# Stationary columns, transpose order and fills in a hand-ordered two-layer decoder kernel

## Chip, cores and metric

The kernel runs on one core of a Trainium2 chip. The metric is device time in microseconds (us) for one launch; lower is better. Engines are named as in the profile: PE is TensorE's matmul side and PEld its weight loads, DVE is VectorE, ACT is ScalarE, POOL is GpSimd, SP is SyncE, which issues the DMAs.

## What is computed

512 tokens and 16 learned meta tokens in front of them (528 rows of width 1024) pass a gated linear attention layer and a differential softmax attention layer. Each layer has an RMS norm, one input projection, a gate and an output projection; a last norm drops the meta rows. The change sits mostly in the first layer, whose core is this (cut from the reference):

```python
def gla_chunk(S, inp):
    q, k, v, lg = inp
    b = jnp.cumsum(lg, axis=2)
    ...
    attn = jnp.einsum('bhid,bhjd,bhijd->bhij', q, k, decay)
    o = (jnp.einsum('bhij,bhjv->bhiv', attn, v)
         + jnp.einsum('bhid,bhdv->bhiv', q * jnp.exp(b), S))
...
q, k, v, z, g_lr = jnp.split(proj, ...)
lg = jax.nn.log_sigmoid((g_lr @ w_gate_up + b_gate)) / GLA_TAU
...
o = head_rms(o) * gnorm
y = jax.nn.silu(z) * o
return y @ w_out
```

There are four heads with keys of 256 and values of 512. In the second layer eight heads of 2 x 128 take a softmax over earlier tokens with a relative bias, the difference of two softmaxes weighs the values, and the same norm, gate and output projection follow.

## The kernel before, in words

**Layout.** Activations lie transposed, features on the 128 partitions and tokens along the row. The 528 tokens are one meta block of 16 and four blocks of 128 (`BLK`). Projections are done in float32r with each operand split in a high and a low part (`split`, L237: ACT copies the high part, DVE subtracts it from the source), three products each. From the second head on, the projections use a seven-product scheme on 2 x 2 blocks (`Unit`, L362); head 0 uses `plain_unit` (L739).

**The order of the work.** PE's order is written out by hand; the other engines are ordered by a scheduler that keeps dependences and favours functions marked `urgent`. `Weaver` (L73) holds a queue of generators, the projections. Each yields the microseconds that it is taken to cost: `Unit` yields 0.33 after three products, `plain_unit` 0.66 after six, the output projection (L821) 0.68 after six. `W.fill(us)` runs yields until their sum reaches `us`; in that way projections are put between the steps of the attention, so that PE has work while DVE and ACT prepare the next step. `W.defer(us, fn)` keeps `fn` until yields of that sum have passed. `W.finish` empties the queue up to `W.stop`, `W.settle` runs what is still deferred. `Weights` (L129) loads weight pieces with SP and has ACT and DVE split them; it looks two pieces ahead.

**One head of the first layer.** `gla_scores` (L1011) scales the keys into `kd` on DVE, multiplies the meta block's keys and queries (L1023, the "meta scores"), then the four diagonal blocks (L1030). Four calls of `gla_cross` (L1038, called from `gla_ready`, L1059, with a fill of 1.5 between) multiply each block's queries by the earlier blocks' keys: at L1048, for each earlier block `j` two products, `j = 0` being the meta block. These score products are in float32; each is carried out as two matmul instructions. L1052 then scales `kd` by the block's decay on DVE. `gla_blocks` (L1066) multiplies the scores by the values (`output`), norms them, and `rows` (L1105) transposes the rows back at L1111.

**Values.** A finished projection tile of the values has features on partitions and has to be turned: `turned_back` (L758) defers a `post` that calls `to_tokens` (L730). That makes one transpose of a 32-column tile for the meta rows (L734) and four of 128 columns (L736), in two tiles of a PSUM pool of four (`ps_tile`). The copies out of them are `split` and `split3` (L328; L333, L334 on ACT, L336, L338 on DVE). `to_tokens` is used by the second layer too (`turned_back2`, L1379), and there the 32-column transposes of the probabilities (L1487) come after the 128-column ones (L1486).

**The branch.** If a decay is very steep, scores are made in another way (`steep_scores`). Whether that is so is found once: DVE reduces the decays to a flag `fl` (L908, L909), a one-column product on PE (L1130, the "steepness product") carries it to PSUM, DVE casts it to `fi` (L1131), and all engines load it and branch (L1133, L1134). The fills around it are at L1128 and L1132. With these inputs the branch is not taken. At that place the queue holds head 0's plain projections of q and k and behind them its gate projection.

Of the kernel before, what the change touches and what calls it, by code (L numbers as in the profile page):

```python
# [19 lines left out]
P = 128  # L20
D = 1024
NM = 16
# [162 lines left out]
def trunk(ctx, tc, x, meta, g_norm, gla_w_in, gla_w_gate_up, gla_b_gate, gla_gnorm, gla_w_out,  # L185
# [3 lines left out]
    act, dve, pe, pool, sp = nc.scalar, nc.vector, nc.tensor, nc.gpsimd, nc.sync  # L189
# [17 lines left out]
    def T(p, shape, dt, tag, **kw):  # L207
        uid[0] += 1
        return p.tile(shape, dt, tag=tag, name=f"{tag}_{uid[0]}", **kw)
# [10 lines left out]
    def ps_tile():  # L220
        return T(ps_pool, [P, 512], F32, "ps")
# [4 lines left out]
    def h2(t):  # L226
        return t.rearrange("p (a b) -> p a b", a=2)
# [44 lines left out]
    W = Weaver()  # L272
# [14 lines left out]
    def want_unit(w, c0):  # L287
        def single(tag, b):
            def fn(raw):
                t = [T(wp, [P, 512], F32R, tag + part, bufs=1) for part in "hl"]  # L290
                split(*t, raw[:, b, :])
                return t
            return Part(tag, fn)

        def add(o, a, b):
            dve.tensor_tensor(o, a, b, op=ALU.add)

        def sums(raw):
            t = T(wp, [P, 2, 512], F32, "sum", bufs=1)
            add(t[:, 1, :], raw[:, 2, :], raw[:, 3, :])  # L300
            add(t[:, 0, :], t[:, 1, :], raw[:, 0, :])
            add(raw[:, 2, :], raw[:, 2, :], raw[:, 0, :])
            return t

        def outer(raw):
            add(raw[:, 1, :], raw[:, 1, :], su.t[:, 0, :])
            ws.room["sum"] += 1
            return block_pair(raw[:, 1:3, :])

        a11, a12, a22 = single("a11", 0), single("a12", 1), single("a22", 3)  # L310
        su = Part("sum", sums)
        s21 = Part("pair", lambda raw: block_pair(su.t))
        s43 = Part("pair", outer)
        ws.want((w, c0), [a11, su, s21, a12, s43, a22])
        return a11, a12, a22, s21, s43
# [174 lines left out]
    def tmp():  # L490
        return T(tp, [P, L], F32, "t")
# [16 lines left out]
    ident = cp.tile([P, P], F32, name="ident")  # L508
# [90 lines left out]
    pm = pm0[:, :KT * NM].rearrange("p (k m) -> p k m", k=KT)  # L599
# [50 lines left out]
    for k0 in range(0, KT, 2):  # L650
        if k0 + 2 < KT:
            scaled_pair(k0 + 2)
        i, ks = k0 // 4, slice(k0 % 4, k0 % 4 + 2)
# [76 lines left out]
    def to_tokens(vt, blocks, short_cols):  # L730


        pt, pm = ps_tile(), ps_tile()[:32, :P]
        pe.transpose(pm, short_cols, ident)  # L734
        for b, (t0, n) in enumerate(blocks[1:]):
            pe.transpose(pt[:, b * P:(b + 1) * P], vt[:, t0:t0 + n], ident)  # L736
        return pt, pm

    def plain_unit(u, evac):  # L739
# [15 lines left out]
    def q_gla_v(hd, s):  # L755
        us = [want_unit(g_w_in, 2048 + 512 * hd + c) for c in (0, 256)] if hd else v_first

        def turned_back(m, vt):  # L758
            def post():
                pt, pm = to_tokens(vt, BLK, vt[:, :32])  # L760
                cs = slice(m * P, (m + 1) * P)
                split(s.v[0][:, :, cs], s.v[1][:, :, cs], pt.rearrange("p (b c) -> p b c", b=4))
                split3(s.vm[:, cs], pm, 32, short[:, NM:NM + 1])
            W.defer(1.4, post)

        gens = []
        for h, u in enumerate(us):
            vts = []

            def dst(h=h, vts=vts):  # L770
                if h == 0:
                    s.vm = T(gp, [M3, 512], F32R, "vm0")
                    s.v = [T(gp, [P, 4, 512], F32R, f"v{i}") for i in range(2)]
                vts.extend([tmp(), tmp()])
                return vts

            if hd:
                gens.append(W.add(Unit(u, X, 1.0, dst, lambda i, h=h, vts=vts: turned_back(2 * h + i, vts[i]))))
            else:
                def evac(i, banks, h=h, vts=vts, dst=dst):  # L780
                    if i == 0:
                        dst()
                    for n, bank in enumerate(banks):
                        act.activation(vts[i][:, n * HT:(n + 1) * HT], bank[:, :HT], AF.Copy)
                    turned_back(2 * h + i, vts[i])

                gens.append(W.add(plain_unit(u, evac)))
        return gens[0]
# [59 lines left out]
    for k in range(KT):  # L848
        for n in range(2):
            for i, x in enumerate((X["b11"], b12) if k < 4 else (X["b21"], X["b22"])):  # L850
                pe.matmul(pgs[i][:112, :HT], glr[:, k, :], x[n][:, k % 4, :],
                          start=k == 0 and n == 0, stop=k == KT - 1 and n == 1)
# [157 lines left out]
    @urgent  # L1010
    def gla_scores(hd, s):  # L1011
        s.a = [T(gp, [P, NR], F32R, f"a{i}") for i in range(2)]
        s.kd = T(gp, [P, 2, 400], F32, "kd")
        for i in range(2):
            dve.tensor_scalar(s.kd[:, i, :NM], s.ks[:, i, :NM], eL[:, 2 * hd + i, 0:1], None, op0=ALU.mult)
            dve.tensor_tensor(s.kd[:, i, NM:].rearrange("p (b c) -> p b c", b=3),
                              s.ks[:, i, NM:400].rearrange("p (b c) -> p b c", b=3),
                              eL[:, 2 * hd + i, 1:4].unsqueeze(2).to_broadcast([P, 3, P]), op=ALU.mult)
        sp.dma_start(s.kd, steep_dr[hd][1], cond=steep > 0, cond_hint=False)
        s.am = T(gp, [M3, NM], F32R, "am")  # L1020
        pm = ps_tile()[:32, :NM]
        for i in range(2):
            pe.matmul(pm, s.ks[:, i, :32], s.qs[:, i, :NM], start=i == 0, stop=i == 1)  # L1023
        r = tmp()
        dve.tensor_tensor(r[:32, :NM], pm, short[:, :NM], op=ALU.mult)
        ps = ps_tile()
        for b in range(4):
            cs = slice(NM + b * P, NM + (b + 1) * P)
            for i in range(2):
                pe.matmul(ps[:, b * P:(b + 1) * P], s.ks[:, i, cs], s.qs[:, i, cs], start=i == 0, stop=i == 1)  # L1030
        dve.tensor_tensor(r[:, NM:].rearrange("p (b c) -> p b c", b=4), ps.rearrange("p (b c) -> p b c", b=4),
                          tri.unsqueeze(1).to_broadcast([P, 4, P]), op=ALU.mult)
        sp.dma_start(r, steep_dr[hd][0], cond=steep > 0, cond_hint=False)
        split3(s.am, r[:32, :NM], 64)
        split(s.a[0], s.a[1], r[:, NM:])

    @urgent
    def gla_cross(hd, s, b):  # L1038


        t0, n = BLK[b]
        ps, w = ps_tile(), (b - 1) * P
        pm = ps[:32, 384:]
        for j in range(b):
            c0 = BLK[j][0]
            o, kc = (ps[:, (j - 1) * P:j * P], slice(c0, c0 + P)) if j else (pm, slice(0, 32))
            for i in range(2):
                pe.matmul(o, s.kd[:, i, kc], s.qs[:, i, t0:t0 + n], start=i == 0, stop=i == 1)  # L1048
        if b < 4:
            for i in range(2):  # L1050
                kd = s.kd[:, i, :t0]
                dve.tensor_scalar(kd, kd, eL[:, 2 * hd + i, b:b + 1], None, op0=ALU.mult)  # L1052
        cs = slice((b - 1) * P, b * P)
        split3(s.cm[:, cs], pm, 64)
        if b > 1:
            cs = slice(w * (b - 2) // 2, w * b // 2)
            split(s.c[0][:, cs], s.c[1][:, cs], ps[:, :w])
# [67 lines left out]
        W.fill(2.0)  # L1125
        rows(4, prev)

    W.fill(1.0)  # L1128
    pf = ps_tile()
    pe.matmul(pf[0:1, 0:1], fl[:, 1:2], one1, start=True, stop=True)  # L1130
    dve.tensor_copy(fi, pf[0:1, 0:1])  # L1131
# [11 lines left out]
    for hd in range(G_HEADS):  # L1143
        s = heads[hd]
        last = hd == G_HEADS - 1
        if hd:
            if not last:
                q_gla_out(hd - 1, heads[hd - 1])
            for half in range(2):
                q_gla_z(hd, s, half)  # L1150
            if not last:
                W.stop = q_gla_qk(hd + 1, heads[hd + 1])[0]
            if hd == 1:
                second_layer_setup()
            W.fill(4.0)
        if hd == 0:
            W.fill(2.0)
        gla_scores(hd, s)
        W.fill(5.0)
        gla_ready(hd, s)  # L1160
        if hd == 0:
            hot = T(gp, [P, TLEN], F32, "kd")
            sp.dma_start(hot[:NBUCK + 1], c_hot)
        W.finish()
        W.settle()
        if hd == 0:
            for m in range(4):
                gla_gate(0, s, m, h2(s.z[:, m, :]))
        if hd == 0:
            q_gla_qk(1, heads[1])  # L1170
        W.stop = None
        if last:
            q_gla_out(hd - 1, heads[hd - 1])
        else:
            W.stop = q_gla_v(hd + 1, heads[hd + 1])
        gla_blocks(hd, s, (1.2, 1.2) if last else (1.7, 1.5), last)
        W.finish()
        W.stop = None

# [427 lines left out]
    s = heads[0]  # L1607
# [14 lines left out]
    for hd in range(D_HEADS):  # L1622
        last = hd == D_HEADS - 1
        s = heads[hd]
# [112 lines left out]
```

## Time and profile before

| | |
|---|---|
| median of 3 timed runs | 1003.09 us (1002.08 to 1003.71) |
| the profiled execution, first to last instruction | 999.6 us |
| the profiled execution's time beyond that span | not recorded apart; the timed median is 3.5 us above the span |
| granted TensorE clock, mean | 0.997 |
| first layer in the timeline | to about 480 us; second layer from there |
| instructions | 18267 |

In a row of the timeline the columns are the start in us, the busy time, engine, line and operation, output and inputs, shape and the number of merged instructions; a bracket gives the idle time ahead of it and what ended that. For a matmul the first shape (128*32) is the stationary operand, partitions by columns, and the second the moving one. Matmuls are pipelined: a single one lasts longer than the distance to the next, so of n merged ones the last starts one duration ahead of the row's end. In a row of the waits the columns are the total in us, how often, and the longest. A row that groups the instructions of one line gives their count and the minimum, median and maximum duration in ns.

### The profile page before, as it was taken

The numbers are of one execution on the slowest core, as the hardware profiler recorded it, in microseconds if no ns is written. First come the engines' busy times: TensorE is split into PE (matmuls) and PEld (weight loads), VectorE is DVE, ScalarE is ACT, GpSimd is POOL, SyncE is SP. The second block draws the span as 40 slices with busy tenths as digits, with TensorE's granted clock in tenths as the row PEclk, the third lists the DMA queues.
The fourth block names the chain that finished last, engine by engine and source line by source line (L and its number), as shares of the span: only waits on it lengthen the run. The fifth ranks groups of instructions, "written<-read, shape, count | busy, mean of one in ns | idle before, by whom it ended". The sixth has DMA issues, their size and how long they took to land.

```text
span 999.6 us, 18267 instructions
## 1 busy us (share of the span) xinstructions
PE 981.0 (98%) x7143; PEld 920.2 (92%) x7143; DVE 784.1 (78%) x1586; ACT 597.5 (60%) x1304; POOL 46.6 (5%) x68
## 2 busy tenths in 40 slices
PE   8999999999999999999999999999999999999997
PEld 6998999999999989999899898899998999988896
DVE  7998886777777787556998886888966879777785
ACT  7775755265535656536567666466664666645583
POOL 1000000001000100000000100000010010000001
PEclk9999999999999999999999999999999999999998
DMA  7322322141233322222231322333222332323212
GB/s 194 82 69 64 86 85 86 48 113 52 85 85 85 85 54 74 86 85 79 84 104 49 94 82 95 85 96 85 85 96 72 87 91 70 109 64 92 85 65 84
DMA packets 121161, 84.24 MB, mean 84 GB/s; under 512 B 6365, under 2 KB 110077, under 8 KB 121072
## 3 DMA queue, kind: packets, MB, share of 16 engines
q1 hardware_dynamic: 121072, 83.05, 28.8%
q8 instruction: 56, 0.92, 0.4%
q14 instruction: 33, 0.27, 0.1%
HBM read 83.64 MB, written 2.12 MB: 86 GB/s over the span
## 4 chain that ended last, share of the span: by engine, by line
PE 78%; DVE 6%; ACT 3%; DMA 3%; issue 1%; POOL 1%; SPq 0%; POOLq 0%; DVEq 0%; ACTq 0%
PE bx L357 15%; PE bx L347 10%; PE bv L357 9%; PE by L357 8%; PE ps L326 7%; PE bx L830 4%; PE bx L326 3%; PE bv L830 2%; PE by L830 2%; DMA raw<-in_gla_w_in_dram 2%; PE ps L1048 2%; PE by L326 2%; PE bv L326 2%; DVE wl L241 1%; PE by L347 1%
## 5 line engine op out<-in xcount | busy, mean ns | idle before, releaser
L240 ACT ACTIVATE wh<-raw 128x1024 fp32r<-128x1024 f32 x99 | 104.4, 1055 | 61.6 <-PE by L830 26.8
L241 DVE TENSOR_TENSOR wl<-raw,wh 128x1024 fp32r<-128x1024 f32 x99 | 121.0, 1222 | 22.0 <-ACT wh L240 14.6
L357 PE MATMUL bv<-x,wh 128*128 128x264 f32 (+1 forms) x656 | 97.5, 286 | 0.0
L357 PE MATMUL bx<-x,wh 128*128 128x264 f32 (+1 forms) x640 | 95.6, 286 | 1.2 <-ACT u L378 1.2
L357 PEld LDWEIGHTS bx<-x,wh 128*128 128x128 f32 x640 | 84.8, 188 | 2.3 <-ACT u L378 1.4
L357 PEld LDWEIGHTS bv<-x,wh 128*128 128x128 f32 x656 | 86.4, 189 | 0.3
L241 DVE TENSOR_TENSOR wl<-sum,wh 128x1024 fp32r<-128x1024 f32 x41 | 50.1, 1222 | 21.0 <-ACT wh L240 17.6
L378 ACT ACTIVATE u<-bx 128x264 f32<-128x264 f32 (+1 forms) x120 | 45.5, 380 | 33.1 <-PE bx L357 29.2
L347 PE MATMUL bx<-x,wh 128*128 128x512 f32 (+1 forms) x256 | 62.4, 385 | 0.0
L1473 ACT ACTIVATE p<-p,st 128x528 f32<-128x528 f32 (+3 forms) x64 | 36.4, 569 | 40.0 <-DVE st L1471 39.9
L357 PE MATMUL bv<-x,wl 128*128 128x264 f32 (+1 forms) x328 | 56.4, 286 | 0.0
L240 ACT ACTIVATE wh<-sum 128x1024 fp32r<-128x1024 f32 x41 | 43.2, 1055 | 19.2 <-PE by L830 9.6
L357 PE MATMUL bx<-x,wl 128*128 128x264 f32 (+1 forms) x320 | 54.5, 285 | 0.0
L347 PEld LDWEIGHTS bx<-x,wh 128*128 128x128 f32 x256 | 44.5, 188 | 7.9
L1509 POOL TENSOR_TENSOR st<-st,mhalf 128x1 f32<-128x1 f32 x32 | 26.5, 828 | 474.9 <-ACT on L1507 426.9
L357 PE MATMUL by<-x,a12h 128*128 128x264 f32 (+1 forms) x320 | 46.9, 285 | 0.0
L357 PEld LDWEIGHTS bv<-x,wl 128*128 128x128 f32 x328 | 46.2, 189 | 0.0
L357 PE MATMUL bx<-x,a11h 128*128 128x264 f32 (+1 forms) x320 | 46.2, 285 | 0.0
L357 PEld LDWEIGHTS bx<-x,wl 128*128 128x128 f32 x320 | 45.3, 188 | 0.1
L240 ACT ACTIVATE a11h<-raw 128x512 fp32r<-128x512 f32 x41 | 25.7, 628 | 32.6 <-DMA raw<-in_diff_w_in_dram 18.2
L357 PEld LDWEIGHTS bx<-x,a11h 128*128 128x128 f32 x320 | 42.2, 189 | 0.8
L357 PEld LDWEIGHTS by<-x,a12h 128*128 128x128 f32 x320 | 41.9, 188 | 0.2 <-issue 0.2
(465 smaller groups left out, 2643.4 us busy)
## 6 DMA issues: line engine op xcount, KB each, us to landing
raw<-in_gla_w_in_dram SPq DMA_DIRECT2D x48, 512.0 KB, 5.3
raw<-in_diff_w_in_dram SPq DMA_DIRECT2D x42, 512.0 KB, 4.2
raw<-in_diff_w_in_dram SPq DMA_DIRECT2D x11, 1024.0 KB, 5.7
raw<-in_gla_w_out_dram SPq DMA_DIRECT2D x8, 1024.0 KB
raw<-in_diff_w_out_dram SPq DMA_DIRECT2D x8, 1024.0 KB, 4.9
T<-bdr SPq DMA_DIRECT2D x8, 264.0 KB
out_dram<-x SPq DMA_DIRECT2D x8, 256.0 KB, 2.0
kd<-steep SPq DMA_DIRECT2D x4, 400.0 KB
```

The source lines that it names most:

```text
L240: act.activation(hi, src, AF.Copy)
L241: dve.tensor_tensor(lo, src, hi.bitcast(F32), op=ALU.subtract)
L326: pe.matmul(ps, l, r, start=first and n == 0, stop=last and n == 2, **kw)
L347: pe.matmul(bank, a[:, k, :], b[k] if n0 is None else b[k][:, n0 + i * nn:n0 + (i + 1) * nn], start=n == 0 and ks[0] == 0, stop=n == len(t ...
L357: pe.matmul(bank[:, :x[q].shape[2]], w[p][:, k * P:(k + 1) * P], x[q][:, k, :], start=first and i == 0, stop=i == len(PASSES) - 1, skip_gr ...
L378: act.activation(t, self.bx[:, :self.n], AF.Copy, scale=self.sc)
L830: pe.matmul(banks[i][:, :HT], h.t[p][:, k, mm * P:(mm + 1) * P], s.y[q][k][:, i * HT:(i + 1) * HT], start=n == 0, stop=n == len(PASSES) - 1)
L1048: pe.matmul(o, s.kd[:, i, kc], s.qs[:, i, t0:t0 + n], start=i == 0, stop=i == 1)
L1473: act.activation(p[:, :nk], p[:, :nk], AF.Exp, scale=-1.0, bias=st[:, m:m + 1], accum_out=st[:, 2 + m:3 + m])
L1509: pool.tensor_tensor(ms, ms, mhalf[:, :1], op=ALU.pow)
```

## The change

Five edits:

1. `to_tokens`: the 32-column transpose comes after the four 128-column ones. The tiles are allocated in the same order as before.
2. `turned_back`: values of the first layer are turned 2.4 after their projection and not 1.4.
3. `gla_scores` and `gla_cross`: the products with the meta block take 128 stationary columns where they took 32. Their results have 128 rows, of which the same 32 are read on.
4. The fill ahead of the steepness product is 2.4 and was 1.0.
5. The fills around `rows` in heads 0 to 2 are 1.9 and 1.6 and were 1.7 and 1.5.

```diff
         pt, pm = ps_tile(), ps_tile()[:32, :P]
-        pe.transpose(pm, short_cols, ident)
         for b, (t0, n) in enumerate(blocks[1:]):
             pe.transpose(pt[:, b * P:(b + 1) * P], vt[:, t0:t0 + n], ident)
+        pe.transpose(pm, short_cols, ident)
         return pt, pm
...
-            W.defer(1.4, post)
+            W.defer(2.4, post)
...
-        pm = ps_tile()[:32, :NM]
+        pm = ps_tile()[:, :NM]
         for i in range(2):
-            pe.matmul(pm, s.ks[:, i, :32], s.qs[:, i, :NM], start=i == 0, stop=i == 1)
+            pe.matmul(pm, s.ks[:, i, :P], s.qs[:, i, :NM], start=i == 0, stop=i == 1)
+        pm = pm[:32]
...
         for j in range(b):
             c0 = BLK[j][0]
-            o, kc = (ps[:, (j - 1) * P:j * P], slice(c0, c0 + P)) if j else (pm, slice(0, 32))
+            o = ps[:, (j - 1) * P:j * P] if j else ps[:, 384:]
+            kc = slice(c0, c0 + P)
...
-    W.fill(1.0)
+    W.fill(2.4)
     pf = ps_tile()
     pe.matmul(pf[0:1, 0:1], fl[:, 1:2], one1, start=True, stop=True)
...
-        gla_blocks(hd, s, (1.2, 1.2) if last else (1.7, 1.5), last)
+        gla_blocks(hd, s, (1.2, 1.2) if last else (1.9, 1.6), last)
```

## The prediction

> **What bounds the kernel now.** I read the page's busy shares first, then its chain of work that ended last, then the waits of TensorE (PE) and of its weight loads (PEld), and then the timeline at each place that the diff touches.
>
> ```profile
> PE 981.0 (98%) x7143; PEld 920.2 (92%) x7143; DVE 784.1 (78%) x1586; ACT 597.5 (60%) x1304; POOL 46.6 (5%) x68
> PE 78%; DVE 6%; ACT 3%; DMA 3%; issue 1%; POOL 1%; SPq 0%; POOLq 0%; DVEq 0%; ACTq 0%
> ```
>
> PE works 981.0 of 999.6 us and holds 78% of the chain. So time can come only from PE: from the 18.6 us in which it has nothing, or from gaps inside what counts as busy. The waits say which gaps belong to the edited lines:
>
> ```profile
> PEld ps L1048 <- issue: 3.5, 16, 0.6
> PE ps L734 <- DVE t L403: 1.5, 1, 1.5
> PE ps L1130 <- DVE fl L909: 1.1, 1, 1.1
> PE ps L1111 <- ACT t L1089: 0.7, 2, 0.4
> ```
>
> L1048 is the cross-block score product; it has 16 gaps that no other engine causes, one for each head and block. L734 and L1130 each wait once; L1111, the rows' transposes, twice. No other wait of PE lies at an edited line, so the ceiling of the change is some us.
>
> **128 columns in the cross blocks (L1046).** The first block of head 0 has only the 32-column products, the last block of head 3 has four of them and then twelve of 128 columns:
>
> ```profile
> 90.83 0.65 PE L357 MATMUL bx<-x,a11l 128*128 128x264 f32 x4
> 91.41 0.62 PE L1048 MATMUL ps<-qs,kd 128*32 128x128 f32 x4
> 91.97 0.87 PE L357 MATMUL by<-x,a22h 128*128 128x264 f32 x5
> ...
> 380.32 0.65 PE L357 MATMUL bx<-x,wl 128*128 128x264 f32 x4
> 380.90 2.16 PE L1048 MATMUL ps<-qs,kd 128*32 128x128 f32 x16
> 382.81 1.22 PE L357 MATMUL bx<-x,a11h 128*128 128x264 f32 x8
> ```
>
> A product of 264 columns lasts 0.284, and four of them 0.65, so they start every 0.122. The last one ahead of the block starts at 90.83 + 0.65 - 0.28 = 91.20; the block should start at 91.32 and starts at 91.41. Behind it, the four products at 0.11 should let L357 go on at 91.85; it goes on at 91.97, and its second product is late by 0.10 (0.87 for five where 0.77 is due). From the last L357 ahead to the second behind, without the normal step, that is 0.77 + 0.10 = 0.87.
>
> What a 128-column float32 product costs stands in the next rows, the scores of head 0:
>
> ```profile
> 82.76 0.65 PE L357 MATMUL bx<-x,a12l 128*128 128x264 f32 x4
> 83.34 0.30 PE L1023 MATMUL ps<-qs,ks 128*32 128x16 f32 x4
> 83.57 2.05 PE L1030 MATMUL ps<-qs,ks 128*128 128x128 f32 x16
> 85.37 0.85 PE L357 MATMUL by<-x,wh 128*128 128x264 f32 x5
> L1030 PE MATMUL ps<-qs,ks x64: 275/275/377, 83.6 to 362.2; 128*128 128x128 f32 x64
> ```
>
> The last of L1030's sixteen starts at 83.57 + 2.05 - 0.275 = 85.345. The first, right behind 32 columns, lasts 0.10 longer; without that the step is (1.775 - 0.10)/15 = 0.112, against 0.109 for the 32-column form. Leaving to L357 takes 0.03, and 0.085 more at its second product (0.85 for five, where 0.77 is due). Entering a float32 product of 128 columns from float32r products, the kind of L357 and L347, is seen once:
>
> ```profile
> 476.39 0.40 PE L347 MATMUL bx<-y,wh 128*128 128x512 f32 x1
> 476.62 0.40 PE L347 MATMUL bx<-v,wh 128*128 128x512 f32 x1
> 476.86 1.02 PE L1243 MATMUL ps<-t,ones 128*128 128x512 f32 x2
> ```
>
> 0.24 after a step of 0.23: no delay. So the first block becomes 0.122 + 3 x 0.112 + 0.03 + 0.085 = 0.57, a gain of **0.30**. The last block takes 382.81 - 380.69 + 0.085 = 2.205 now, and 0.122 + 15 x 0.112 + 0.03 + 0.085 = 1.92 then: 0.29, here through the switch inside the block. Sixteen blocks give **4.8 us**, all on PE's path. The bounds: if the late entry (0.09, and 0.02 in the first step) belongs to float32 and not to the columns, 16 x 0.11 = 1.8 stays and 3.0 is left. A loss would need the 128-column loads unhidden, a rival below. I take the L1243 row, as it is the transition itself.
>
> The same rows give L1022. From the last L357 ahead (83.13) to the first behind is 2.24; twenty products at 0.112 make 0.122 + 19 x 0.112 + 0.03 = 2.28. What the clean switches save is eaten by the 16-column products, which now step by 0.112 and not by 0.03: 4 x 0.04, **a loss of 0.2 us**.
>
> [...]
>
> **Steepness fill (L1128).**
>
> ```profile
> 74.97 0.77 PE L747 MATMUL bx<-x,wl 128*128 128x264 f32 x5
> 76.59 0.15 DVE L909 TENSOR_SCALAR fl<-fl 128x1 f32<-128x1 f32 x1
> 76.80 0.19 PE L1130 MATMUL ps<-ones,fl 128*1 128x1 f32 x2 [1.07 <-DVE fl L909]
> 77.38 1.23 DVE L241 TENSOR_TENSOR wl<-sum,wh 128x1024 fp32r<-128x1024 f32 x1 [0.21 <-ACT wh L240]
> ```
>
> The last L747 starts at 74.97 + 0.77 - 0.28 = 75.46, and PE then waits for DVE's `fl` until 76.80. The work filled in comes in yields of 0.66 for six products: 1.0 lets two through, 2.4 four. Twelve more products take 12 x 0.122 = 1.46, so L1130 comes at about 77.1, after `fl`. What stays is the switch to one column (0.21 from start to start by the entries above). Gain 76.80 - 75.46 - 0.21 = **1.1 us**. It is no less unless DVE's cast of the flag falls behind the 1.23 us subtraction at 77.38; PE's branch then comes late, and about 0.6 is given back. The next fill of 1.5 still puts 15 products between flag and branch (18 before), three of them from the gate projection. Behind the branch and the finish that follows it, the same 64 yields and one of the gate projection have been issued as before, so nothing later changes place. On DVE the two evacuations of k now come ahead of its branch, not behind; SP, whose loads stand behind its own branch, passes it 0.3 later.
>
> **Values' defer (L764).** 1.4 lets five yields of 0.33 pass, 2.4 eight: nine products, 1.1 us; in head 0 one yield of 0.66 more, 0.7 us. Of sixteen posts only these stall:
>
> ```profile
> 42.17 0.27 PE L734 MATMUL ps<-ident,t 128*32 128x128 f32 x1
> 42.42 0.88 PE L736 MATMUL ps<-ident,t 128*128 128x128 f32 x4
> 43.06 0.37 PE L747 MATMUL bv<-x,wl 128*128 128x264 f32 x1
> ...
> 369.27 0.43 DVE L403 SCALAR_TENSOR_TENSOR t<-by,u 128x264 f32<-128x264 f32 x1
> 369.76 0.28 PE L734 MATMUL ps<-ident,t 128*32 128x128 f32 x1 [1.46 <-DVE t L403]
> 372.30 0.36 DVE L1052 TENSOR_SCALAR kd<-kd,eL 128x16 f32<-128x16 f32 x2
> 373.03 0.66 PE L736 MATMUL ps<-ident,t 128*128 128x128 f32 x4 [0.22 <-DVE cm L336]
> 374.45 1.24 PE L1048 MATMUL ps<-qs,kd 128*32 128x128 f32 x8 [0.39 <-DVE v L241]
> 358.00:384.00 26.00, 23.93 (x192) 21.82 (x191) 23.66 (x49) 13.29 (x32) 0.00 (x0) 1.00 0.30 81
> ```
>
> In head 0 five transposes take 0.89 from first start to the next product, where 5 x 0.11 are due: 0.34, with the late start **0.4**, gone. In head 3 PE stood about 1.6 for `t`; with the new count the first cross block and three yields (0.6 + 1.1 = 1.7) come ahead of that post, so the wait just closes. The next two waits (0.4 each) are for DVE, which is busy 23.66 of 26 us there (behind the window and its length, the row has busy time and count of PE, PEld, DVE, ACT and POOL). Late next is L1052: it scales `kd` for the second cross block, which will be asked for about 3 us sooner. So I count the first wait, **1.6**, and neither of the others; the bounds are 0 and 2.5. Beside the other twelve posts PE does not wait, and the values are read a stage later.
>
> **Rows' fill (L1176).** In these stages all fills are yields of 0.33: 1.7 and 1.9 both let six through, 1.5 and 1.6 both five. The order of the work is the same: **0**, and L1111's 0.7 us stay.
>
> **32-column transposes last (L734).**
>
> ```profile
> 35.29 0.27 PE L734 MATMUL ps<-ident,t 128*32 128x128 f32 x1
> 35.40 0.60 PE L736 MATMUL ps<-ident,t 128*128 128x128 f32 x4
> 35.75 0.85 PE L747 MATMUL bx<-x,wl 128*128 128x264 f32 x5
> ...
> 542.05 0.49 PE L1486 MATMUL ps<-ident,p 128*128 128x128 f32 x3
> 542.38 0.27 PE L1487 MATMUL ps<-ident,p 128*32 128x128 f32 x1
> 542.40 0.85 PE L357 MATMUL by<-x,a22h 128*128 128x264 f32 x5
> ```
>
> First or last, a 32-column transpose takes its 0.11, and the product behind starts 0.03 later and runs five in 0.85. **0.** In the second layer ScalarE starts on the short tile 0.44 us later; it idles 40% of the span, and the values wait for a later stage. Without that cover it is 16 x 0.44 = 7 us on ScalarE, not on PE.
>
> **Sum.** 4.8 - 0.2 + 1.1 + 0.4 + 1.6 = 7.7 us, made against the profiled span of 999.6. The three timed runs have a median of 1003.09, 3.5 above that span, which lies outside of the first and last instruction and stays. 1003.1 - 7.7 = **995.4 us**.
>
> **Rivals.** (a) The late entry is float32's: 1.8 less, 997.2. For it: every late entry seen is float32; against it: L1243. (b) Head 3's wait moves to L1052 or to the values' tiles instead of going, and the branch's cast falls behind: 2.2 less, and up to 1.5 of new waits from DVE's other order: 997.6 to 999.1. For it: DVE at 91% there. (c) The long loads come bare: 64 x (0.112 - 0.03) = 5.2 back, 1000.6. Against it: steps of 0.109 and 0.112. (d) PE does not get faster, since PE's time is set by something that no row shows: 1003. (e) Slower: the posts now sit beside the cross blocks, two tiles of the four-tile PSUM pool each, and their copies queue on DVE ahead of L1052. If each of the six pairs of posts of heads 1 to 3 then costs the 1.6 seen once, 9.7 come on, and 1003.1 - 5.7 + 9.7 = 1007.1. It decides from 5.7/6 = 0.95 us per pair. Against it: five pairs show no wait now.
>
> **Chances.** Forecast 0.62, (a) 0.10, (b) 0.13, (c) 0.04, (d) 0.04, (e) 0.07. A measurement of this kernel tells about 0.2%, 2 us, from no change. Forecast, (a), (b) and (c) are faster: 0.89; (d) the same: 0.04; (e) slower: 0.07. The low end takes in 2.5 in head 3 and small gains of my rounding, 993; the high end (b) and (c), 1000.6.
>
> **What would show it.** Right: the 16 "issue" waits of L1048 gone, and its blocks starting 0.12 after L357; L1130 without a wait; L734 without one in head 3; L1111's waits as before. Wrong: L1048 late by 0.09 still (a), new waits of PE on L1052, L338 or L241 between 360 and 380 us (b, e), or L1048 steps over 0.12 (c).

## The result, and the profile after

| | before | changed |
|---|---|---|
| median of the timed runs, same chip | 1002.59 us (4 runs) | **996.91 us** (995.75 to 998.37, 4 runs) |
| ratio | | **0.9945**, 95% interval 0.9929 to 0.9961 |
| a second set of runs of both, later | 1003.19 us (11 runs) | 997.77 us (5 runs), ratio 0.9944 (0.9929 to 0.9958) |
| profiled execution, first to last instruction | 999.6 us | 996.6 us, own time 998.37 |

The change is faster by 5.4 to 5.7 us; the sum had said 7.7. The time of 995.4 is 1.5 too low, inside its range.

Lines in the changed kernel: L734 and L736 are now L736 (32 columns) and L735 (128 columns), L1023 keeps its number, L1030 is L1031, L1048 is L1050, L1052 is L1054, L1111 is L1113, L1130 is L1132, L1131 is L1133, L1134 is L1136. First the busy shares of the changed kernel's page:

```profile
PE 979.5 (98%) x7143; PEld 925.1 (93%) x7143; DVE 783.2 (79%) x1586; ACT 596.7 (60%) x1304; POOL 48.3 (5%) x68
```

TensorE (PE) is busy 1.5 us less with the same 7143 matmuls. The chain of this trace was followed back over only 7% of the span, so nothing is read from it. The waits of the changed kernel (total us, times, longest):

```profile
PE by L357 <- PEq L1136: 1.5, 1, 1.5
PE ps L1113 <- ACT t L1091: 0.7, 2, 0.4
PE ps L736 <- DVE v L241: 0.6, 1, 0.6
PE ps L326 <- DVE aT L241: 0.4, 1, 0.4
PE ps L326 <- DVE v L241: 0.4, 2, 0.2
PE ps L1050 <- DVE kd L1054: 0.2, 1, 0.2
```

The 16 "issue" gaps of the cross blocks are gone, and so are the flag product's wait and the values' 1.5. The rows' 0.7 stays. New are 1.5 at PE's own branch and four small waits for DVE. Of these the one of 0.4 for `aT` belongs to this execution: e11, the same kernel run again, has none.

**Where the time went, stage by stage.** The two programs issue almost the same matmuls, so they can be laid side by side: start of a matmul in the trace of before, less the start of the same one in the other trace, is the other kernel's lead. The table gives what the lead grew by in each stage (medians over the matmuls within 1.2 us of the stage's ends, which are times of before's trace):

| kernel | 0 to 33 | 33 to 90: first posts, flag, branch | 90 to 366: heads 0 to 2 | 366 to 395: head 3 | 395 to 990 | 33 to the end |
|---|---|---|---|---|---|---|
| changed | -2.18 | -0.13 | 3.40 | 2.34 | -1.02 | **4.59** |
| e11: changed, again | -1.91 | -0.33 | 3.01 | 2.26 | -0.26 | **4.68** |
| e1: columns alone | -1.90 | 0.16 | 3.19 | 0.91 | 0.29 | 4.55 |
| e2: flag fill alone | -0.88 | -0.23 | -0.33 | 0.28 | -0.16 | -0.44 |
| e3: defer alone | -2.38 | -0.39 | -0.30 | 1.69 | 0.10 | 1.10 |
| e4: short last alone | -1.14 | -0.52 | -0.19 | 0.06 | -0.30 | -0.95 |
| e5: changed, short first | -1.75 | -2.41 | 3.17 | 2.28 | -0.34 | 2.70 |
| e6: both fills alone | -1.11 | 0.60 | 0.05 | 0.19 | -0.27 | 0.57 |
| e7: column probe | -1.27 | 0.22 | 0.94 | 0.92 | -0.44 | 1.64 |
| e8: rows' fill alone | -0.93 | 0.32 | -0.11 | -0.01 | -0.94 | -0.74 |
| e9: changed, cast on ScalarE | -0.95 | 0.92 | 3.02 | 2.45 | -2.04 | 4.35 |
| e10: changed, both fills | -0.04 | 0.71 | 3.31 | 2.33 | -0.23 | **6.12** |
| e12: as e10, short first | -1.28 | -0.47 | 3.40 | 2.19 | 0.05 | 5.17 |

e8 runs the same order of instructions as before, so its row is the method's own scatter: 0.3 in a stage, 0.9 in the long last one. e1, e7 and e8 leave the stage up to the branch as it was, and have 0.16 to 0.32 there, so the zero of that column is at about 0.2. The first column belongs to the execution and not to the kernel: before's and the changed kernel's orders are the same on every engine up to 35 us. It goes with the granted clock (PEclk) between 16 and 26 us; the window's row of before and of the changed kernel:

```profile
16.00:26.00 10.00, 8.36 (x55) 6.95 (x55) 9.85 (x14) 6.67 (x12) 0.00 (x0) 1.00 0.59 102
```
```profile
16.00:26.00 10.00, 8.53 (x36) 7.20 (x36) 9.85 (x14) 6.67 (x12) 0.00 (x0) 0.67 0.63 100
```

The profiled execution of before had the full clock there, 1.00; with 0.67 the changed one starts 2.2 us behind; e10, with 1.00 as well, starts level. So the leads are counted from 33 us.

**The columns.** The products ahead of and behind head 0's meta and first scores, then its first cross block and the last block of head 3, in the changed kernel's timeline:

```profile
85.08 0.65 PE L357 MATMUL bx<-x,a12l 128*128 128x264 f32 x4
...
87.71 1.21 PE L357 MATMUL by<-x,wh 128*128 128x264 f32 x8
...
93.14 0.65 PE L357 MATMUL bx<-x,a11l 128*128 128x264 f32 x4
93.63 0.60 PE L1050 MATMUL ps<-qs,kd 128*128 128x128 f32 x4
93.99 0.37 PE L357 MATMUL by<-x,a22h 128*128 128x264 f32 x1
...
377.07 0.65 PE L357 MATMUL bx<-x,wl 128*128 128x264 f32 x4
377.56 2.04 PE L1050 MATMUL ps<-qs,kd 128*128 128x128 f32 x16
379.35 1.22 PE L357 MATMUL bx<-x,a11h 128*128 128x264 f32 x8
```

The last L357 ahead of the first block starts at 93.14 + 0.65 - 0.28 = 93.51 and the block at 93.63: 0.12, no late entry. Over the 16 blocks the entry is 0.119 to 0.124, with one exception of 0.48, head 3's second block, and 14 of the blocks agree with the prediction's steps within 0.01 us (the last one is 0.08 longer). Added up, the 16 blocks are 4.7 us shorter than in before, and 4.8 in e1. The scores' stretch, from start to start, is 87.71 - (85.08 + 0.65 - 0.28) = 2.26 long; it was 2.24.

**The flag and the branch** of the changed kernel:

```profile
79.26 0.19 PE L1132 MATMUL ps<-ones,fl 128*1 128x1 f32 x2
79.29 1.23 DVE L241 TENSOR_TENSOR wl<-sum,wh 128x1024 fp32r<-128x1024 f32 x1 [0.64 <-ACT wh L240]
80.43 1.25 DVE L241 TENSOR_TENSOR x<-y,x 128x1056 fp32r<-128x1056 f32 x1
80.94 0.53 PE L357 MATMUL by<-x,a11h 128*128 128x264 f32 x3
81.60 0.14 DVE L1133 CAST fi<-ps 1x1 int32<-1x1 f32 x1
82.94 0.84 PE L357 MATMUL by<-x,a11h 128*128 128x264 f32 x5 [1.47 <-PEq L1136]
```

The flag's sum is in PSUM by about 79.45. Two subtractions are ahead of the cast on DVE, which is at 81.60. PE has run dry at 81.47, and takes its first matmul behind the branch at 82.94, 1.20 after the cast's end. What the wait for `fl` gave is paid again 3 us later.

**Head 3**, the posts and the second cross block of the changed kernel:

```profile
369.06 0.27 PE L736 MATMUL ps<-ident,t 128*32 128x128 f32 x1
369.09 0.97 PE L357 MATMUL by<-x,a12h 128*128 128x264 f32 x6
370.26 1.16 PE L1050 MATMUL ps<-qs,kd 128*128 128x128 f32 x8 [0.20 <-DVE kd L1054]
...
373.17 0.28 PE L736 MATMUL ps<-ident,t 128*32 128x128 f32 x1 [0.59 <-DVE v L241]
```

The wait of 1.46 for `t` is gone; 0.20 for `kd` and 0.59 at the next post came in its place, of which the latter was 0.22 and 0.39 in two places before.

**The second layer.** Beside a post, in the changed kernel and then at the same place in before:

```profile
546.50 0.68 DVE L241 TENSOR_TENSOR v<-ps,v 128x512 fp32r<-128x512 f32 x1
547.21 0.34 DVE L338 SCALAR_TENSOR_TENSOR vm<-ps,short,vm 32x128 fp32r<-32x128 f32 x1
547.24 0.63 PE L326 MATMUL ps<-v,aT 128*128 128x256 f32 x3 [0.19 <-DVE v L241]
```
```profile
550.06 0.34 DVE L338 SCALAR_TENSOR_TENSOR vm<-ps,short,vm 32x128 fp32r<-32x128 f32 x1
550.46 0.97 PE L326 MATMUL ps<-v,aT 128*128 128x256 f32 x6
550.73 0.69 DVE L241 TENSOR_TENSOR v<-ps,v 128x512 fp32r<-128x512 f32 x1 [0.33 <-ACT v L240]
```

DVE's order has turned with the transposes': the 0.68 us subtraction of 512 columns now runs ahead of the short 0.34, and L326 starts 0.06 after its end. In before L326 started 0.06 after the end of the short one, ahead of the subtraction. Which of the two it needs is not shown.

### The profile page after: what moved, and what is told of

The parts are those of the page before. It is cut to its first block, busy times and chain, and to the rows that moved or that the text cites. A ratio compares the mean times of both kernels' runs of the same rounds, so it can differ in the third digit from the quotient of the medians.

```text
span 996.6 us, 18277 instructions
## 1 busy us (share of the span) xinstructions
PE 979.5 (98%) x7143; PEld 925.1 (93%) x7143; DVE 783.2 (79%) x1586; ACT 596.7 (60%) x1304; POOL 48.3 (5%) x68
## 5 line engine op out<-in xcount | busy, mean ns | idle before, releaser
L357 PE MATMUL bv<-x,wh 128*128 128x264 f32 (+1 forms) x656 | 97.3, 287 | 0.0
L357 PE MATMUL bx<-x,wh 128*128 128x264 f32 (+1 forms) x640 | 95.2, 286 | 1.0 <-ACT u L378 1.0
L357 PEld LDWEIGHTS bv<-x,wh 128*128 128x128 f32 x656 | 86.3, 189 | 0.3
L357 PEld LDWEIGHTS bx<-x,wh 128*128 128x128 f32 x640 | 84.6, 188 | 2.0 <-ACT u L378 1.5
L357 PE MATMUL bv<-x,wl 128*128 128x264 f32 (+1 forms) x328 | 56.4, 286 | 0.0
L357 PE MATMUL bx<-x,wl 128*128 128x264 f32 (+1 forms) x320 | 54.6, 285 | 0.0
L357 PE MATMUL by<-x,a12h 128*128 128x264 f32 (+1 forms) x320 | 46.5, 285 | 0.0
L357 PEld LDWEIGHTS bv<-x,wl 128*128 128x128 f32 x328 | 46.2, 189 | 0.1
L357 PE MATMUL bx<-x,a11h 128*128 128x264 f32 (+1 forms) x320 | 46.2, 285 | 0.0
L357 PEld LDWEIGHTS bx<-x,wl 128*128 128x128 f32 x320 | 45.3, 188 | 0.1
L357 PEld LDWEIGHTS bx<-x,a11h 128*128 128x128 f32 x320 | 42.3, 189 | 0.8
L357 PEld LDWEIGHTS by<-x,a12h 128*128 128x128 f32 x320 | 41.7, 188 | 0.0
```

Of the source, the lines that this page charges most:

```text
L357: pe.matmul(bank[:, :x[q].shape[2]], w[p][:, k * P:(k + 1) * P], x[q][:, k, :], start=first and i == 0, stop=i == len(PASSES) - 1, skip_gr ...
```

## The experiments

The theory after the result: the columns carry nearly all of the gain; the flag's fill gains nothing, because the cast is late on DVE and the branch stands; the defer gains its 1.6 in head 3; the transposes' order costs some tenths. The rivals were that the late entry is float32's (then the gain would come from elsewhere), and that the branch stands for want of products, whoever casts.

**Columns alone (e1).** Before with the diff's lines at L1021 and L1046 only; those at L1046:

```
-            o, kc = (ps[:, (j - 1) * P:j * P], slice(c0, c0 + P)) if j else (pm, slice(0, 32))
+            o = ps[:, (j - 1) * P:j * P] if j else ps[:, 384:]
+            kc = slice(c0, c0 + P)
```

> The kernel before with only the 128 stationary columns in gla_scores and gla_cross. Theory: TensorE stands at each change between a float32 product of 32 columns and one of 128; the sixteen cross blocks save 0.30 us each and the four score stages lose 0.03 to 0.04, so PE is 4.6 to 4.8 us ahead behind head 3, and the time falls by 4 to 5 us (ratio 0.995 to 0.996). Rival: the gain of the whole change comes from the defer and the fill, and the columns give half of it (3.0 us, the late entry stays) or less; then L1048 still starts 0.21 behind the product ahead of it.

998.72 us (5 runs, before 1002.36), ratio 0.9962 (0.9948 to 0.9975), aligned 4.55 us. The columns alone give as much as the whole change does in its two traces, 4.59 and 4.68. The medians show less of it, 3.6 us against 5.4 to 5.7; the intervals of the ratios overlap. Of the 4.55, 0.16 and 0.29 lie in stages without a cross block, where e8 scatters as much; the two stages that have them give 3.19 + 0.91 = 4.10. That is less than the 4.8 of the blocks. In head 3 a wait beside them has grown (L736 for `cm`: 0.6, in before 0.2); in heads 0 to 2 the kernels without wide columns lie between -0.33 and 0.05.

**How many columns stand (e7).** Before with 48, 64, 80 and 96 meta columns in heads 0 to 3, to see which of these counts still cost the 0.30 a block; the columns past 32 are not used:

```
+        nc0 = (48, 64, 80, 96)[hd]
...
+            o, kc = (ps[:, (j - 1) * P:j * P], slice(c0, c0 + P)) if j else (ps[:nc0, 384:], slice(0, nc0))
```

> The kernel before with 48, 64, 80 and 96 stationary columns in the meta products of gla_cross in heads 0, 1, 2 and 3. [...]

A first block with 48 columns, a second one with 64 and one with 80:

```profile
91.88 0.65 PE L357 MATMUL bx<-x,a11l 128*128 128x264 f32 x4
92.46 0.64 PE L1049 MATMUL ps<-qs,kd 128*48 128x128 f32 x4
...
165.09 0.28 PE L357 MATMUL bx<-x,a22l 128*128 128x264 f32 x1
165.31 1.29 PE L1049 MATMUL ps<-qs,kd 128*64 128x128 f32 x8
...
266.36 0.61 PE L357 MATMUL bv<-x,wh 128*128 128x264 f32 x3
266.81 1.05 PE L1049 MATMUL ps<-qs,kd 128*80 128x128 f32 x8
```

From the last L357's start to the block's: 92.46 - 92.25 = 0.21, 165.31 - 165.09 = 0.22, and 266.81 - (266.36 + 0.61 - 0.28) = 0.12. Whole blocks of 48 and 64 columns are 0.31 to 0.33 longer than the steps of 128 columns make them, those of 80 and 96 within 0.03 of them, but for one that waits for DVE. So 64 columns stand and 80 don't: the gain is the columns' and not float32's. Why the border lies between 64 and 80 is not shown by any row; only the border and the price are.

**The flag's fill alone (e2).** `W.fill(1.0)` at L1128 becomes `W.fill(2.4)`.

> The kernel before with only the fill ahead of the flag's product raised from 1.0 to 2.4. Theory: the wait of 1.1 us at L1130 goes, but DVE has the cast of the flag queued behind two subtractions of 1.2 us, so PE stands 1.4 to 1.7 us at the branch instead, and PE is 0.0 to 0.3 us behind at the first scores (L1023). Rival: the branch's wait in the changed kernel came from the other edits' order of work, and alone the fill gives 1.1 us at L1023.

1002.71 us in one run. In its trace the cast stands behind the same two subtractions, 2.4 after the flag's product (77.99):

```profile
80.41 0.14 DVE L1131 CAST fi<-ps 1x1 int32<-1x1 f32 x1
81.75 0.84 PE L357 MATMUL by<-x,a11h 128*128 128x264 f32 x5 [1.55 <-PEq L1134]
```

The lead grows by 1.5 up to the products behind the flag's and falls by 1.8 at the branch. The fill alone is worth nothing.

**The second fill as well (e6).** Before with 2.4 and, between cast and branch, 3.0 for 1.5.

> The kernel before with the fill ahead of the flag's product at 2.4 and the fill between it and the branch at 3.0 instead of 1.5 (30 products between flag and branch and not 15). Theory: what costs at the branch is PE waiting for the cast that DVE has queued behind two subtractions, so 1.8 us more of products hide it and PE is 1.0 to 1.3 us ahead at the first scores (L1023). Rival: the branch itself costs PE that time (refilling its queue, or a register load that goes out late whatever DVE does); then it stands 1.4 us again, only later.

1001.86 us in one run. The stand at the branch fell to 0.17, with 0.27 for k's evacuation (L724), and behind the branch the trace keeps 0.60 (0.57 at the end) where 1.0 to 1.3 was expected. The mechanism holds, its size is about half, or less by that column's zero.

**Who casts (e9), more work behind the cast (e10), and the changed kernel once more (e11)**, side by side on one chip. e9 and e10 change one line each of the changed kernel:

```
-    dve.tensor_copy(fi, pf[0:1, 0:1])
+    act.copy(fi, pf[0:1, 0:1])
```
```
-    W.fill(1.5)
+    W.fill(3.0)
     steep = nc.values_load(fi[0:1, 0:1], min_val=0, max_val=P)
```

> The changed kernel with one line other: the cast of the steepness flag is made by ScalarE and not by VectorE. TensorE's and POOL's orders are the same; on ScalarE the cast stands behind the 1.07 us copy at 79.16 and so should run at about 80.3, not at 81.60 behind VectorE's two subtractions. Theory (TensorE stands 1.5 us at its branch for the cast's place on VectorE): the stand falls from 1.5 to about 0.2, and the aligned gain over the changed kernel right behind the branch is about 1.3 us; k's two evacuations now come behind VectorE's branch and may give up to 0.4 of it back, so the median is some 0.9 to 1.3 us under the changed kernel of the same call. Rival (the branch is late for the fewer products between flag and branch, or for the branch's own latency, whoever makes the cast): the stand stays 1.0 to 1.5 and the time that of the changed kernel.

> The changed kernel with the second fill, between cast and branch, at 3.0 in place of 1.5. Theory (TensorE only lacks work to cover the cast's late place): the stand at the branch falls from 1.5 to 0.2, as in the run that had both fills alone, and 0.5 to 1.2 us stay at the end, so the median is that much under the changed kernel of the same call. Rival (the other static order that the longer fill gives VectorE costs what the stand cost): the stand goes, and waits of TensorE for VectorE of the same sum come in the heads behind; the time is that of the changed kernel within 0.3 us.

> The changed kernel itself, for the two beside it, on the same chip. It should repeat: 996 to 998 us at the median, ratio 0.993 to 0.996 to the kernel before, with a span of about 1.8 us less than the time. If it comes out over 1 us from its first median, differences of 1 us between kernels of different calls can't be read from medians at all, and only the aligned traces count.

| | median, us | runs | ratio to before | 95% interval |
|---|---|---|---|---|
| e9, cast on ScalarE | 996.55 | 6 (994.5 to 997.47) | 0.9928 | 0.9912 to 0.9943 |
| e10, both fills | **995.54** | 5 (995.2 to 997.49) | 0.9929 | 0.9913 to 0.9944 |
| e11, changed, again | 997.77 | 5 (997.05 to 998.29) | 0.9944 | 0.9929 to 0.9958 |

e9's cast and branch, then e10's:

```profile
78.93 0.13 ACT L1133 CAST fi<-ps 1x1 int32<-1x1 f32 x1
79.23 1.25 DVE L241 TENSOR_TENSOR x<-y,x 128x1056 fp32r<-128x1056 f32 x1
79.70 0.53 PE L357 MATMUL by<-x,a11h 128*128 128x264 f32 x3
80.37 0.85 PE L357 MATMUL by<-x,a11h 128*128 128x264 f32 x5 [0.15 <-PEq L1136]
```
```profile
79.45 0.14 DVE L1133 CAST fi<-ps 1x1 int32<-1x1 f32 x1
80.59 0.99 PE L357 MATMUL bx<-x,a12h 128*128 128x264 f32 x6 [0.20 <-DVE ks L724]
81.75 0.48 PE L357 MATMUL bx<-x,a12h 128*128 128x264 f32 x2 [0.18 <-PEq L1136]
```

In e9 the same PE program, with the same 15 products between flag and branch, stands 0.15 and not 1.5 to 1.7: the cast runs 0.9 after the flag's product (78.02) instead of 2.3, ahead of DVE's second subtraction. So it is the cast's place on DVE, and the rival falls. In e10 the cast is as late, and more products cover it. Both stages from 33 to 90 us are about 1 us better than the changed kernel's. In e9 the trace loses that again after 395 us (-2.04), where its program has the changed one's order on every engine. The largest part of it, 0.93, is scatter of the execution. It falls at one place of the second layer, where POOL raises one column to a power and ScalarE and then PE's L1516 (L1518 in the changed kernels) wait for it. That operation in before, in e8 and in e9:

```profile
562.18 1.17 POOL L1509 TENSOR_TENSOR st<-st,mhalf 128x1 f32<-128x1 f32 x1 [7.18 <-ACT on L1507]
562.95 1.81 POOL L1509 TENSOR_TENSOR st<-st,mhalf 128x1 f32<-128x1 f32 x1 [7.17 <-ACT on L1507]
556.72 2.45 POOL L1511 TENSOR_TENSOR st<-st,mhalf 128x1 f32<-128x1 f32 x1 [7.18 <-ACT on L1509]
```

In nine of the 14 traces it lasts 1.16 or 1.17 and the lead stays within 0.04; in four 1.80 or 1.81, and 0.28 to 0.53 is lost (the changed kernel's first trace and e8, in before's own order, among them); in e9 2.45. The rest of e9's loss is the 0.45 of the transposes and some 0.7 at waits near 920 us, of which no cause is shown. e10 keeps its gain: 6.12 against 4.59 and 4.68.

The medians of e9 and e10 are 1.2 and 2.2 us under that of e11 beside them, with intervals of the ratios that overlap, and by the ratio e9 and e10 are level. That e10's lead is more than the 1.0 of this stage goes with the clock: three of its five runs have a mean granted clock of 0.999, none of e11's has more than 0.997. The changed kernel's one run at 0.999 took 995.75, e10's three 995.2 to 995.54, e9's two 994.5 and 995.01. So both are likely, but not surely, ahead of the changed one, and which of them is faster is open.

**The defer alone (e3).** `W.defer(1.4, post)` becomes `W.defer(2.4, post)`.

> The kernel before with only the values' transposes of the first layer deferred by 2.4 instead of 1.4. Theory: the wait of 1.5 us at 369.8 goes, a wait of about 0.5 us for the tiles stays or comes back behind it, and PE is 1.0 us ahead at the last head's rows, nothing before that head. Rival: the 1.0 us seen in head 3 came from the shorter cross blocks that shift PE against DVE; then the defer alone gives less than 0.3 us.

1002.07 us in one run. Head 3 gives 1.69 with all its new waits counted, the term's 1.6. But 0.39 is lost up to the branch, where head 0's 0.4 should have been gained (PE's wait for `fl` is 1.6 and was 1.1), as DVE's flag comes 0.5 later; the -0.30 in heads 0 to 2 is no more than e2 has there (-0.33). That makes 1.10 in all for the 2.0 forecast.

**The short transposes last, alone (e4)**, and **first again in the changed kernel (e5)**.

```
-        pe.transpose(pm, short_cols, ident)
         for b, (t0, n) in enumerate(blocks[1:]):
             pe.transpose(pt[:, b * P:(b + 1) * P], vt[:, t0:t0 + n], ident)
+        pe.transpose(pm, short_cols, ident)
```

> The kernel before with only the 32-column transposes moved behind the 128-column ones in to_tokens. Theory: nothing in the first layer (within 0.2 us), and 0.5 to 1.0 us lost in the second layer, at single waits of the values' products (L326) for DVE, since ScalarE and DVE get the short tile later and their order changes. Rival: the 1.0 us lost there in the changed kernel comes from the shift of PE against the others; then PE at the end is within 0.2 us of before.

> The changed kernel with the 32-column transposes first again, as before. Theory: moving them cost about 0.9 us, spread over head 0's post, the flag and single waits of the second layer; so PE ends 0.7 to 1.1 us further ahead of the kernel before than the changed kernel does (4.5 us once the start is taken out), the ratio near 0.9945. Rival: what was lost in the second layer of the changed kernel comes from PE being earlier; then the end stays within 0.3 us of the changed kernel's.

e4 took 1003.49 us in one run; its trace loses 0.95. Two of its waits:

```profile
PE ps L1130 <- DVE fl L909: 1.5, 1, 1.5
PE ps L326 <- DVE v L241: 0.4, 2, 0.2
```

0.52 goes up to the branch (the flag comes 0.4 later than in before), and 0.45 in the second layer, in two steps near 550 and 600 us. The size is near the expected one, the place only half.

e5, which should have won that back, came out **slower** than the changed kernel: 999.44 us (5 runs, before 1002.80), ratio 0.9960 (0.9946 to 0.9974, which overlaps the changed kernel's), aligned 2.70. Neither theory had that. Its branch and the window behind it:

```profile
81.91 0.14 DVE L1133 CAST fi<-ps 1x1 int32<-1x1 f32 x1
83.25 1.14 PE L357 MATMUL by<-x,a11h 128*128 128x264 f32 x5 [2.03 <-PEq L1136]
```
```profile
83.20:87.00 3.80, 3.75 (x18) 3.79 (x19) 3.65 (x8) 1.02 (x2) 0.00 (x0) 0.55 0.06 13
```

PE stood 2.03 us, 0.5 more than in the changed kernel, and then ran 3.8 us at a granted clock of 0.55, with 18 matmuls where the changed kernel had 34 at 1.00. About 1.5 us is lost there, for a stand only 0.5 longer. Whether all of its runs had that stretch is not shown: three took 999.44 to 1000.31 us at a mean clock of 0.993 to 0.995, the other two 997.57 and 998.04 at 0.997.

**Short first with the branch covered (e12).** e10 with the transposes first: does the second layer come back, and does the flag's stage still lose?

> The changed kernel with the second fill at 3.0, as in e10_both_fills, and its 32-column transposes first again. The second layer is where every kernel with these transposes last loses 0.18 us near 550 us and 0.21 to 0.26 near 600 us against the kernel before, with two waits L326 <- DVE v L241 of 0.2 each, and no kernel with them first has either. Theory (the loss of 0.45 us belongs to the order of the transposes; the loss of the run with them first was the uncovered branch alone): both waits are gone, the aligned loss between 545 and 615 us falls by about 0.45, the branch stands at most 0.4, no stretch of half clock follows it, and the net aligned gain is 6.0 to 7.0 us; median 994.5 to 996. Rival (with the transposes first VectorE's order at the flag costs TensorE whatever covers the branch): the flag's stretch from 74 to 90 us loses 1 us or more against e10_both_fills, and the time is 996.5 or over.

996.76 us (5 runs, before 1002.90), ratio 0.9938 (0.9925 to 0.9952), aligned 5.17. Its waits near the flag:

```profile
PE bx L357 <- DVE ks L724: 0.7, 1, 0.7
PE ps L1132 <- DVE fl L909: 0.3, 1, 0.3
PE bx L357 <- PEq L1136: 0.2, 1, 0.2
```

Each theory was half right. The second layer's loss is gone: between 545 and 615 us the five kernels with these transposes last lose 0.40 to 0.45, in the same two places; e12 loses none, and no stretch of half clock follows. But up to the branch it is 1.2 us behind e10 (-0.47 against 0.71), with waits for `fl` and for k's evacuation that e10 has not or smaller, and its time is over the rival's bound of 996.5. In before's fills the same edit cost 0.5 of that stage (e4), here its opposite costs 1.2: what it does to DVE's order ahead of the flag depends on the fills, and no sign of its own was found.

**The rows' fills alone (e8).** 1.7 and 1.5 become 1.9 and 1.6.

> The kernel before with only the fills around the rows' transposes at 1.9 and 1.6. Theory: the yields of 0.33 make six and five steps as before, so the program is the same, and the time is within what two runs of one kernel differ by (ratio 0.998 to 1.002); this also shows how far profiles of one program lie apart. Rival: the fills move work and L1111's waits fall by some of their 0.7 us.

1002.96 us (10 runs), before 1002.80, ratio 1.000 (0.999 to 1.0009). Nothing, as forecast.

## Why the prediction was right in sign and too large

**Columns, 4.8: right.** Entry, step and exit came out as worked out, 0.57 for the first block, and the L1243 row decided rightly against rival (a). The blocks themselves are 4.7 us shorter (4.8 in e1). With the meta scores, of the 4.6 forecast 4.10 are seen in the stages that hold them, and 4.55 in the whole trace of e1. Rivals (c) and (d) fall with it. A load of 128 columns is the longer one, 0.19 (mean of the 160 of L1050) against 0.11 with 32 (mean of the 64 of L1048 in before), but the 128-column products still start every 0.112.

**Meta scores, -0.2: half**, -0.02 each, -0.1 in all.

**Steepness fill, 1.1: the step that failed.** The prediction named the condition itself: "no less unless DVE's cast of the flag falls behind the 1.23 us subtraction". It did, behind that one and a second of 1.25, and the price was not 0.6 but all of it: the stage from 33 to 90 us gave -0.13 and -0.33 (about 0.2 less by that column's zero) where 1.1 and head 0's 0.4 were counted. Two things were missed. The order of the engines is fixed when the program is built, so a product that comes later by a yield takes its reader on DVE past work that was behind it. And 1.20 us pass from the cast's end to PE's first matmul behind the branch (81.74 to 82.94, in e2 80.55 to 81.75, in e5 82.05 to 83.25). The cover of 15 products, 15 x 0.122 = 1.83, is enough for the product, a prompt cast and the branch, as e9 shows, and not for 1.4 more.

**Values' defer, 2.0: half.** The 1.6 of head 3 is there (1.69 alone; 2.34 - 0.91 = 1.43 beside the columns), with L1052 late next by 0.20, as named. The prediction said that no other wait of PE lies at an edited line; its own rows further down show two, L736's 0.22 and L1048's 0.39, and 0.59 of the two stayed. Head 0's 0.4 is not, because the stall was put down to the transposes and belonged to what they waited for. In before they waited at 42.42 and 42.75 for DVE's L887 and ScalarE's L784. In the changed kernel the posts lie elsewhere, and the product L881, which ran at 39.73 in before and did not wait, waits for the same L887:

```profile
41.91 0.75 PE L881 MATMUL ps<-a,z 128*128 128x264 f32 x2
```

These two take 0.60 from the first start to the next product (42.51), where 0.24 are due. So the stall has moved, and at 75 us, ahead of the flag's product, the lead has grown by 0.05 (changed, e11) and 0.12 (e3) and not by 0.4. In e3 the flag then comes 0.5 later. Rival (b) happened in part: the cast fell behind, and 0.59 for the values' tiles and 0.20 for L1052 stand in head 3, waits that the prediction had named as signs that it was wrong.

**Rows' fill, 0: right** (e8).

**32-column transposes last, 0: wrong by 0.45** in the second layer. The cover was named as "the values wait for a later stage"; but it is DVE and not ScalarE that counts, whose order of the two subtractions turned, and L326 starts behind the longer one where it started behind the shorter.

**Rival (e), slower: no.** The posts beside the cross blocks cost one wait of 0.20 and one of 0.59 in head 3, and heads 0 to 2 none that shows.

**The base.** The 3.5 us between span and median were said to lie outside of the first and last instruction. 1.8 do (own time 998.37, span 996.6); the other 1.7 is the spread of executions: the profiled one of before had the full clock at its start, and of the 13 traces set beside it all but e10's start 0.9 to 2.4 behind it. It takes nothing from the difference, but it makes single traces unfit for differences under 2 us unless they are counted from behind the start.

Without the failed terms (1.1, 0.4 and 0.45) the sum would have been 7.7 - 1.95 = 5.75; timed were 5.4 to 5.7, aligned 4.6. That the time agrees so well with 5.75 is partly luck, as one start moves it by up to 2 us; and 996.9 lies nearest to rival (a)'s 997.2, which the entries of 0.12 rule out. The sum of the five parts run alone is 4.55 - 0.44 + 1.10 - 0.95 - 0.74 = 3.5, and 4.3 without e8's scatter: the parts add within that scatter.

## What to carry to other kernels

A wait that is closed by putting work ahead of it has to be followed to the end of its chain: here the flag's product, its cast on another engine, the register load and the branch; the price stands where the engine next runs dry. Read the order of the reader's engine for it: a small, urgent operation behind two large ones on a static queue was here better moved to another engine (e9, a stand of 0.15 for 1.47) or covered with more work (e10, 0.20 and 0.18). And gaps that are small and regular, 16 times 0.30 from one cause, are the safer forecast than single waits of 1 us: the former came out to the hundredth, the latter half.

## What the runs showed of the hardware

- Float32 products with 32 (before), 48 or 64 stationary columns (e7) amid 128-column ones cost 0.28 to 0.33 us for the way in and out (0.09 at the entry, the rest behind); with 80, 96 (e7) and 128 (the changed kernel, entry 0.12) they don't. The transposes of 32 columns show no stand: in the changed kernel L736 at 369.06 and the L357 behind it at 369.09 start 0.03 apart, as a 128-column product would be left.
- A stand of 2.03 us was followed by 3.4 us of half clock (in e5 from about 83.6, since the slice 83 to 84 has a PEclk of 0.80 and those from 84 to 87 have 0.50, to 87.0). Behind the changed kernel's stand of 1.47 the clock was 1.00 (82.94 to 90), and behind the stands of 1.55 (e2) and 1.67 (e11) the four products with `a11l` took 0.64 and 0.65, where they took 1.08 in e5.
- The length without work alone does not tell whether the clock falls. Between 16 and 20 us TensorE had 1.40 us without work in before and 1.41 in the changed kernel. In before the clock stayed at 1.00; in the changed kernel it was 0.66 from 19 to 20, 0.50 from 20 to 26 and 0.93 from 26 to 27, so about 6.8 us at a half. What sets it off is not shown.
- Executions with the same order of work differ by up to 2.4 us in their first 33 us (before against e3), with the granted clock between 0.67 and 1.00 from 16 to 26 us. That is more than any single edit of this change is worth but the columns.
- One and the same one-column power on POOL lasted 1.16 to 1.17 (1.17 in before), 1.80 to 1.81 (1.81 in e8) or 2.45 us (e9), and TensorE lost up to 0.93 us by it.
